# A hybrid decoder step: the side work beside the attention at other steps of the matrix engine's order, and two reciprocal roots on GpSimd

## The chip, the cores and the metric

The kernel runs on one core of a Trainium2 chip. The metric is the device time of one execution in microseconds (us). The kernel before took 2998.84 us (median of 3 runs, from 2991.91 to 3001.22 us). The engines are named as the profile names them: PE (TensorE's matmuls) with PEld (its weight loads), DVE (VectorE), ACT (ScalarE), POOL (GpSimd), and SP (SyncE), which here only issues DMAs, in the order of its program. Each engine works through its own list of instructions in order and waits at an instruction until what that one needs is there.

## The reference

One layer of a decoder for 2048 new prompt tokens and for a "sample" of 8 requests with 4 tokens each. Cut to what matters here:

```python
proj = rmsnorm(x, norm_attn_g) @ w_in               # 1024 -> 7 x 512
o_a  = HGRN2(qa, fa, ia)                            # gated recurrence, 4 heads of 128
o_a  = rmsnorm(o_a, hgrn_onorm_g) * silu(ga)        # needs 1/sqrt(mean(o_a^2) + EPS)
o_b  = dilated_attn(qb, kb, vb)                     # 8 heads of 64, windows (128,1), (512,4), (2048,16)
h    = x + concat(o_a, o_b) @ w_o
h    = h + ConvFFN(rmsnorm(h))                      # 1024 -> 2816 -> 1024
h    = h + sigmoid(rmsnorm(h) @ w_ple_gate) * (p @ w_ple_proj)
y    = rmsnorm(h)
```

The sample's tokens attend to a cached window of keys and values, and their recurrence starts from a stored state of 4 x 128 x 128 numbers for each request. Prompt and sample share the weights.

## The kernel before, in words

The program has three stages. First come the input projections for two blocks of tokens, with the prompt's recurrence (`hgrn_unit`, seven of its eight units) between them. Then comes the attention of the prompt, some 360 us, with the "side work" beside it. Last comes the trunk (output projection, channel mixer, embeddings), which takes the rest, about 1800 us.

The change touches the middle stage. The prompt's attention, `attn_phase`, is a generator that yields once per step. It goes through four pairs of heads (p = 0 to 3), and 160 units of 128 queries. Step x issues: the scores of unit x (lines 814 and 815: S from the query tile `qS` and the high and low part of the keys, `kH` and `kL`); on DVE the mask and the row's extreme (line 819), on ACT the exponential (line 820); at every second step, for the two units before, the transposes (line 827, `PT`), their copies on DVE or ACT (829) and the products with the values (839, `acc`). At planned steps it also issues the next pair's operands: `stage` (line 693, DMAs of a quarter of q and k), and and `stack`, which splits them: POOL rounds and subtracts (`qS` 152 and 704, `kL` 708), ACT casts (`kH` 707). `merge` (lines 745 to 778) reads row statistics back from memory, makes coefficients (DVE 753, 759; POOL 754 to 760; ACT 755, 765), writes and reads them back (`coef_d`, `cf`) and blends two results on POOL (775, 777).

The side work, `others()`, is a second generator with 92 steps: 31 of the recurrence's last unit (`hgrn_unit(..., apart=True)`), 44 of the sample's attention (`attn_sample`) and 17 of the sample's recurrence (`hgrn_sample`). `attn_sample` works on two groups of four requests. Each group streams 16 tiles (`skt`) from memory, through four buffers: eight of keys (line 944: four `kT_w`, four `kT_d`) and then eight of values (line 983: `v_w`, `v_d`), one tile per step, each with one product of PE (946, 986); between them stand a few steps of softmax and transposes without a tile. `hgrn_sample` loads one request's state per step (646), multiplies (659, 662), updates it on DVE (665) and writes it back (667).

A "turn" is one step of the attention, and after it, at some turns, one step of the side work. Within this loop PE's order is the order in which the code issues it (`manual_schedule` for PE). The other engines' order is made by a scheduler with a model of time; `first(side, 1)` issues the side's step with raised priority. Before the change the side stepped at every turn below 28 and then at every even turn, so its step n of 28 and more stood at turn 28 + 2 (n - 28): the sample's attention at turns 36 to 122, its recurrence at 124 to 156. The loop ends at turn 167.

The recurrence's unit ends with a norm: DVE makes the mean square `o_v` (line 573), `rsqrt_small` makes the reciprocal root of its 128 x 8 numbers by a bit trick and three rounds of Newton's method, eleven small DVE instructions (lines 104 to 109), DVE scales the two heads' output (579), PE transposes it (586). `hgrn_sample` does the same with one column of 128 (`hsv`, lines 671 to 677).

Of the kernel before, what the change touches and what calls it, by code (L numbers as in the profile page):

```python
# [11 lines left out]
F32 = mybir.dt.float32  # L12
# [4 lines left out]
ALU = mybir.AluOpType  # L17
# [31 lines left out]
def hymba_step_kernel(ctx: ExitStack, tc: tile.TileContext, I: dict, O: dict):  # L49
    nc = tc.nc  # L50
    V, A, G, PE, SP = nc.vector, nc.scalar, nc.gpsimd, nc.tensor, nc.sync

    const = ctx.enter_context(tc.tile_pool(name="const", bufs=1))
# [22 lines left out]
    ones = const.tile([128, 128], F32, name="ones")  # L76
    V.memset(ones, 1.0)

    mask = early.tile([128, 768], F32, name="mask")
    qT_s = early.tile([128, 4, NS], F32, name="qT_s")  # L80
    kT_s = early.tile([128, 4, NS], F32, name="kT_s")
# [14 lines left out]

    def f32(ap):
        return ap.bitcast(F32)

    def rsqrt_small(pool, v, shape):  # L100
        i = pool.tile(shape, I32, name="rs_i")
        y = pool.tile(shape, F32, name="rs_y")
        t = pool.tile(shape, F32, name="rs_t")
        V.tensor_scalar(i, v.bitcast(I32), 1, None, op0=ALU.logical_shift_right)
        V.tensor_scalar(y.bitcast(I32), i, -1.0, RSQRT_SEED, op0=ALU.mult, op1=ALU.add)
        for _ in range(3):
            V.tensor_mul(t, y, y)
            V.scalar_tensor_tensor(t, t, -0.5, v, op0=ALU.mult, op1=ALU.mult)
            V.scalar_tensor_tensor(y, t, 1.5, y, op0=ALU.add, op1=ALU.mult)
        return y  # L110
# [72 lines left out]
    def split_to(w, raw):  # L183
        A.copy(w[:, 0], raw)  # L184
        V.tensor_sub(w[:, 1], raw, f32(w[:, 0]))  # L185
        return w
# [3 lines left out]
    def down_weights(pool):  # L190

        tile_ = lambda: pool.tile([128, 512], F32, name="draw", bufs=8)
        for p in range(PAIRS):
            a = [tile_() for _ in range(4)]
            with tc.issue_after(recent[0].ins):
                for x, (i, j) in zip(a, itertools.product(range(2), repeat=2)):
                    SP.dma_start(x, I["w_down"][2 * p + j][:, 512 * i:512 * i + 512])
            for n, raw in factors(*a, tile_):
                w = split_to(pool.tile([128, 2, 512], F32R, name="dw", bufs=3), raw)
                SP.dma_start(f32(wd_d[p][n - 1]), f32(w))  # L200
                yield
# [22 lines left out]
    def in_phase(bi, tiles, shared, wp, ev, sm, pmm, pms, plv, po):  # L224
# [15 lines left out]
        def load_x(k, c0, cn):  # L240
            start = bi == 0 and c0 == 0
            cs = slice(c0, c0 + cn)
            g = gains[:, 0, k:k + 1]
            raw = ev.tile([128, 384], F32, name="xr", bufs=3)[:, :cn]
            SP.dma_start(raw, I["xT"][128 * k:128 * k + 128, t0 + c0:t0 + c0 + cn])
            A.activation(xh[k][:, cs], raw, AF.Copy, scale=g)  # L246
            V.scalar_tensor_tensor(xl[k][:, cs], raw, g, f32(xh[k][:, cs]), op0=ALU.mult, op1=ALU.subtract)  # L247
            if t0 + c0 + cn == NTOK:
                G.tensor_scalar(xs[:, k], raw[:, cn - NS:], g, 1.0, op0=ALU.mult, op1=ALU.mult)
            if k == 0:  # L250
                A.activation(ssq[:, cs], raw, AF.Square)
            else:
                sq = ev.tile([128, 512], F32, name="sg", bufs=2)[:, :cn]
                A.activation(sq, raw, AF.Square)
                (G if start else V).tensor_add(ssq[:, cs], ssq[:, cs], sq)
# [184 lines left out]
    def hgrn_unit(u, heads, S, ld, wk, sp, plv, po, pms, msk, diag, apart=False):  # L440
# [130 lines left out]
            yield  # L571
        v = sp.tile([128, 2, 4], F32, name="o_v")
        V.tensor_scalar(v, ssq, 1.0 / 128, EPS, op0=ALU.mult, op1=ALU.add)
        r = rsqrt_small(sp, v.rearrange("p h c -> p (h c)"), [128, 8])
        if apart:
            yield
        for i, h in enumerate(heads):
# [15 lines left out]
    def hgrn_sample(hp, pps):  # L593
# [76 lines left out]
        v = hp.tile([128, 1], F32, name="hsv")  # L670
        A.activation(o, ops, AF.Square, accum_out=v)
        V.tensor_scalar(v, v, 1.0 / 128, EPS, op0=ALU.mult, op1=ALU.add)
        r = rsqrt_small(hp, v, [128, 1])
        V.tensor_scalar(o, ops, r, None, op0=ALU.mult)
        yield
        pt = pps.tile([128, 4, 128], F32, name="s1")
# [897 lines left out]
    def pools(st, **kw):  # L1574
        def pool(name, bufs, **k):
            return st.enter_context(tc.tile_pool(name=name, bufs=bufs, reuse_waits="tile", **kw, **k))
        return pool

    in_st, hgrn_st, attn_st = [ExitStack() for _ in range(3)]
    pool = pools(in_st)  # L1580
# [11 lines left out]
    def hgrn(lo, hi, *psum, apart=False):  # L1592
        for i in range(lo, hi):
            heads = (0, 1) if i % 2 == 0 else (2, 3)
            yield from hgrn_unit(i // 2, heads, S, ld, wk, sp, *psum, msk, diag, apart)

    def first(gen, n):

        with tc.high_priority(AHEAD):
            return step(gen, n)  # L1600
# [17 lines left out]
    pool = pools(hgrn_st, side="right")  # L1618
    hc, ld, wk, sp = pool("h_c", 1), pool("h_l", 2), pool("h_w", 2), pool("h_s", 2)
# [19 lines left out]
    pool = pools(attn_st)  # L1639
# [5 lines left out]
    def others():  # L1645
        yield from hgrn(7, 8, from_pool(pps, "s1", "s2"), from_pool(pps, "s1"), from_pool(pps, "s2"), apart=True)
        for h in range(4):
            SP.dma_start(O["ps"][h], S[h])
        hgrn_st.close()
        with ExitStack() as st:  # L1650
            pool = pools(st)
            yield from attn_sample(pool("s_c", 1), pool("s_k", 4), pool("s_w", 1), pps)
        with ExitStack() as st:
            yield from hgrn_sample(pools(st)("hsp", 1), pps)

    side = others()
    with tc.manual_schedule(engines={mybir.EngineType.PE}):
        for turn in itertools.count(1):
            if next(main) == "last":
                break  # L1660
            if turn % 2 == 0 or turn < 28:
                first(side, 1)
        first(side, 1000)
    step(main, 1000)
# [4 lines left out]
    with ExitStack() as st:  # L1669
        pool = pools(st)  # L1670
# [9 lines left out]
        tr, tp, dw, ts, th, te, tw, hp = [pool(n, k) for n, k in (  # L1680
            ("tr", 7), ("tp", 6), ("dw", 6), ("ts", 1), ("th", 6), ("te", 2), ("tw", 44), ("thh", 8))]
# [143 lines left out]
```

## Time and profile before

| | before |
|---|---|
| time, median of 3 runs | 2998.84 us |
| the profiled execution's own time | 2996.88 us |
| its span, first to last instruction | 2995.1 us |
| PE busy | 2899.1 us (97 %) |
| DVE, ACT, POOL busy | 2163.4, 1318.4, 674.0 us |
| mean granted PE clock | 0.987 |

The profile is of one execution. Its page gives busy time by engine; the other views (windows, timeline, waits, groups by line, DMA) are answers of the same trace. In the timeline a row reads: start in us, duration in us, engine, line, operation, output<-input, tile sizes, how many instructions are merged; in brackets stands the idle time of the engine just before, and what ended it. In the windows view a row is a stretch of time with each engine's busy time (and its number of instructions), the granted PE clock as a share of full speed, the mean busy share of the 16 DMA engines and the GB/s that they moved. A DMA share at or above 1 means that packets queue up.

### The profile page before, as it was taken

Reading aid. Unit: us, or ns where it says so; the run is one execution under the profiler, and the core shown is the slowest. Engines: PE = TensorE matmul, PEld = TensorE weight load, DVE = VectorE, ACT = ScalarE, POOL = GpSimd, SP = SyncE. Lnnn points to the kernel's source line nnn. Section 1 sums busy time; section 2 is a strip of 40 time slices with the busy share of each in tenths; the row PEclk is TensorE's granted clock in tenths of the full one; section 3 lists DMA queues with packets and bytes.
Section 4 is the critical chain, followed back from the end, with each engine's and each line's share of the span. In section 5 each row is a group of like instructions: output and inputs, shape, how many; then the busy total and the mean of one; then the engine's idle time right before and its main releaser. Section 6 shows DMA issues by size and latency. Waiting matters only on the chain.

```text
span 2995.1 us, 52434 instructions
## 1 busy us (share of the span) xinstructions
PE 2899.1 (97%) x18895; PEld 2700.5 (90%) x18895; DVE 2163.4 (72%) x4717; ACT 1318.4 (44%) x2856; POOL 674.0 (23%) x792
## 2 busy tenths in 40 slices
PE   8999999999989898999999999999999999999998
PEld 8987789887777677999999999999999999999998
DVE  6656758657386467569987888766679777677777
ACT  5333423222276576335444444544444544444443
POOL 1443222212143563103443431000001000000000
PEclk9999999999999999999999999999999999999998
DMA  5898634324349996766766668777779777778773
GB/s 179 297 355 305 206 105 120 99 80 124 123 114 279 249 234 177 258 233 210 243 203 204 203 200 293 236 242 243 252 242 308 251 237 243 245 261 295 267 268 132
DMA packets 342036, 659.88 MB, mean 220 GB/s; under 512 B 62928, under 2 KB 134736, under 8 KB 339984
## 3 DMA queue, kind: packets, MB, share of 16 engines
q1 hardware_dynamic: 304928, 468.42, 49.0%
q0 software_dynamic: 33264, 121.13, 12.8%
q10 hardware_dynamic: 3584, 66.98, 6.2%
q8 instruction: 149, 2.44, 0.3%
q14 instruction: 111, 0.91, 0.1%
HBM read 509.46 MB, written 213.92 MB: 242 GB/s over the span
## 4 chain that ended last, share of the span: by engine, by line
PE 59%; issue 17%; DMA 10%; DVE 9%; POOL 2%; ACT 2%; SPq 1%; POOLq 0%; DVEq 0%; ACTq 0%
PE mm L146 13%; PE mm L148 13%; PE mm L147 13%; PE mm L348 2%; PE mm L349 2%; PE mm L350 2%; POOL w L1296 1%; DMA cf<-coef_d 1%; PE acc L839 1%; PE PT L827 1%; PE S L814 1%; DMA xr<-in_xT_dram 1%; PE lv L485 1%; DVE w L185 1%; DMA draw<-in_w_down_dram 1%
## 5 line engine op out<-in xcount | busy, mean ns | idle before, releaser
L147 PE MATMUL mm<-w 128*128 128x348 f32 (+3 forms) x3636 | 1166.1, 321 | 1.3 <-DVE w L1456 0.8
L146 PE MATMUL mm<-w 128*128 128x348 f32 (+3 forms) x3508 | 1108.7, 323 | 18.7 <-ACT s L1254 6.2
L148 PE MATMUL mm<-w 128*128 128x348 f32 (+3 forms) x3508 | 1117.3, 321 | 2.0 <-DVE w L185 2.0
L147 PEld LDWEIGHTS mm<-w 128*128 128x128 f32 x3636 | 684.1, 188 | 4.1 <-DVE w L1088 2.0
L146 PEld LDWEIGHTS mm<-w 128*128 128x128 f32 x3508 | 656.2, 188 | 26.6 <-ACT s L1254 8.7
L148 PEld LDWEIGHTS mm<-w 128*128 128x128 f32 x3508 | 659.0, 188 | 3.3 <-DVE w L185 2.6
L185 DVE TENSOR_TENSOR w<-raw,w 128x512 fp32r<-128x512 f32 x586 | 421.1, 723 | 176.2 <-ACT w L184 168.6
L184 ACT CAST w<-raw 128x512 fp32r<-128x512 f32 x586 | 360.9, 621 | 413.1 <-PE mm L148 288.8
L1296 POOL DMA_DIRECT2D w<-wd_d x231 | 124.3, 538 | 899.2 <-PE mm L148 793.4
L1312 DVE TENSOR_TENSOR h<-h,mm 128x348 f32<-128x348 f32 (+1 forms) x504 | 247.7, 507 | 44.8 <-PE mm L148 43.5
L820 ACT ACTIVATE P<-P,st 128x256 f32<-128x256 f32 (+3 forms) x256 | 134.0, 526 | 60.0 <-DVE st L819 56.4
L1254 ACT COPY s<-mm 128x348 f32<-128x348 f32 (+1 forms) x198 | 88.0, 445 | 152.2 <-PE mm L148 151.9
L819 DVE CUSTOM_DVE_ANT_0 P<-S,mask 128x256 f32<-128x256 f32 (+3 forms) x256 | 104.4, 448 | 62.0 <-PE S L815 40.2
L348 PE MATMUL mm<-wh,xh 128*128 128x512 f32 x352 | 140.8, 403 | 0.1
L349 PE MATMUL mm<-wl,xh 128*128 128x512 f32 x352 | 140.7, 401 | 0.2 <-DVE wl L271 0.2
L350 PE MATMUL mm<-wh,xl 128*128 128x512 f32 x352 | 140.3, 399 | 0.0
L146 PE MATMUL mm<-xh,wh 128*128 128x384 f32 (+2 forms) x384 | 124.6, 329 | 8.0 <-ACT xh L246 5.2
L148 PE MATMUL mm<-xh,wl 128*128 128x384 f32 (+2 forms) x384 | 124.4, 328 | 4.2 <-DVE wl L271 4.2
L147 PE MATMUL mm<-xl,wh 128*128 128x384 f32 (+2 forms) x384 | 125.0, 328 | 1.2 <-DVE xl L247 1.2
L185 DVE TENSOR_TENSOR dw<-draw,dw 128x512 fp32r<-128x512 f32 x77 | 75.3, 981 | 54.0 <-ACT dw L184 53.6
L152 POOL TENSOR_SCALAR wh<-wraw 128x512 fp32r<-128x512 f32 x96 | 75.3, 798 | 133.3 <-PE mm L147 41.6
L814 PE MATMUL S<-kH,qS 128*128 128x256 f32 (+3 forms) x256 | 98.6, 400 | 6.7 <-DVE st L819 4.2
(346 smaller groups left out, 5053.2 us busy)
## 6 DMA issues: line engine op xcount, KB each, us to landing
w<-wd_d POOLq DMA_DIRECT2D x231, 512.0 KB, 5.5
wd_d<-dw SPq DMA_DIRECT2D x77, 512.0 KB
out_sk_dram<-in_cache_k_dram ACTq DMA_DIRECT2D x56, 584.0 KB
out_sv_dram<-in_cache_v_dram ACTq DMA_DIRECT2D x56, 584.0 KB
raw<-in_w_gate_dram SPq DMA_DIRECT2D x110, 256.0 KB
raw<-in_w_up_dram SPq DMA_DIRECT2D x110, 256.0 KB
wraw<-in_w_in_dram SPq DMA_DIRECT2D x104, 256.0 KB
raw<-w_gate_d SPq DMA_DIRECT2D x88, 256.0 KB
```

The source lines that it names most:

```text
L146: PE.matmul(ps, lhsT=wh, rhs=xh, start=first, stop=False, skip_group_check=read)
L147: PE.matmul(ps, lhsT=wh, rhs=xl, start=False, stop=False, skip_group_check=read)
L148: PE.matmul(ps, lhsT=wl, rhs=xh, start=False, stop=last, skip_group_check=read)
L184: A.copy(w[:, 0], raw)
L185: V.tensor_sub(w[:, 1], raw, f32(w[:, 0]))
L348: PE.matmul(ps, lhsT=xh[k][:, js], rhs=wh, start=k == 0, stop=False)
L349: PE.matmul(ps, lhsT=xh[k][:, js], rhs=wl, start=False, stop=False)
L350: PE.matmul(ps, lhsT=xl[k][:, js], rhs=wh, start=False, stop=k == NK - 1)
L814: PE.matmul(s[:, w * i:w * i + w], lhsT=bl.q(hh), rhs=bl.k(kH, hh), start=True, stop=False)
L820: A.activation(pe, pe, AF.Exp, bias=mn, scale=-1.0, accum_out=st[:, bl.r, hh, 0:1])
L1296: G.dma_start(t, wd_d[p][n - 1])
L1312: V.tensor_add(o, o, acc[m][:, :H])
```

## The change

Three edits. `rsqrt_pow` makes the reciprocal root with one POOL instruction, a power with exponent -0.5 from a constant tile `root`; it is used in `hgrn_sample` and in the recurrence's unit that runs beside the attention (`apart`), while the first seven units keep `rsqrt_small`. And the side work steps, from turn 28 on, at three of seven turns instead of one of two, and above turn 136 at five of seven.

```diff
+    root = const.tile([128, 1], F32, name="root")
+    G.memset(root, -0.5)
...
+    def rsqrt_pow(pool, v, shape):
+        y = pool.tile(shape, F32, name="rs_y")
+        G.tensor_tensor(y, v, root.to_broadcast(shape), op=ALU.pow)
+        return y
...
-        r = rsqrt_small(sp, v.rearrange("p h c -> p (h c)"), [128, 8])
+        r = (rsqrt_pow if apart else rsqrt_small)(sp, v.rearrange("p h c -> p (h c)"), [128, 8])
...
-        r = rsqrt_small(hp, v, [128, 1])
+        r = rsqrt_pow(hp, v, [128, 1])
...
-            if turn % 2 == 0 or turn < 28:
+            if turn < 28 or turn % 7 in (0, 2, 4) or (turn > 136 and turn % 7 in (1, 5)):
                 first(side, 1)
```

By this rule the sample's attention stands at turns 37 to 137 (before 36 to 122) and its recurrence at 138 to 161 (before 124 to 156). The steps of the recurrence's last unit that hold the root stand where they stood. The same PE instructions are issued in another order, and before and behind the attention stage no engine's order changes. From `rsqrt_small` on, the changed kernel's lines are counted higher by 7: the old line 819 is now 826.

The first place is DVE's list at the norm of the recurrence's last unit. Before, the last twelve rows up to the scaling of the two heads (`at`):

```order
L105 TENSOR_SCALAR rs_y<-rs_i 128x8
L829 COPY pt<-PT 128x512
L107 TENSOR_TENSOR rs_t<-rs_y 128x8
L108 SCALAR_TENSOR_TENSOR rs_t<-rs_t,o_v 128x8
L109 SCALAR_TENSOR_TENSOR rs_y<-rs_t,rs_y 128x8
L107 TENSOR_TENSOR rs_t<-rs_y 128x8
L108 SCALAR_TENSOR_TENSOR rs_t<-rs_t,o_v 128x8
L109 SCALAR_TENSOR_TENSOR rs_y<-rs_t,rs_y 128x8
L107 TENSOR_TENSOR rs_t<-rs_y 128x8
L108 SCALAR_TENSOR_TENSOR rs_t<-rs_t,o_v 128x8
L109 SCALAR_TENSOR_TENSOR rs_y<-rs_t,rs_y 128x8
L579 TENSOR_TENSOR at<-at,rs_y 128x512 x2
```

The same place of the change, from the mean square `o_v` on (the ISA rows are the masks and extremes of the attention's scores):

```order
L580 TENSOR_SCALAR o_v<-o_ssq 128x8
L826 ISA P,st<-S,mask 128x256
L826 ISA st 128x1
L826 ISA P,st<-S,mask 128x256
L826 ISA st 128x1
L826 ISA P,st<-S,mask 128x256
L826 ISA st 128x1
L826 ISA P,st<-S,mask 128x256
L826 ISA st 128x1
L836 COPY pt<-PT 128x512
L586 TENSOR_TENSOR at<-at,rs_y 128x512 x2
L594 TENSOR_TENSOR hg<-s_9590,hg 128x512
```

The eleven small instructions are gone, and the scaling stands behind the attention's own rows alone. On POOL one row is new there:

```order
L711 TENSOR_TENSOR qS<-stage,qS 64x512 x2
L761 TENSOR_TENSOR w<-mn,st 128x16
L104 TENSOR_TENSOR rs_y<-o_v,root 128x8
L715 TENSOR_TENSOR kL<-stage,kH 128x4x128 x2
L764 TENSOR_TENSOR wl<-w,st 128x16
```

It stands ahead of the two key differences `kL` of the next pair.

The second place is SP's list where the last two quarters of the fourth pair's operands (`stage`) are fetched. Before:

```order
L983 DMA skt<-in_v_d_dram 96x4x512
L745 DMA st<-stat_d 128x4x4
L693 DMA stage<-qT_d 64x2x512 x2
L737 DMA v<-v_d 32x4x128 x8
L693 DMA stage<-kT_d 64x2x512 x2
L734 DMA v<-v_d 128x4x128
L737 DMA v<-v_d 32x4x128 x2
L693 DMA stage<-qT_d 64x2x512 x2
L737 DMA v<-v_d 32x4x128 x2
L745 DMA st<-stat_d 128x4x4
L693 DMA stage<-kT_d 64x2x512 x2
```

And of the change:

```order
L990 DMA skt<-in_v_w_dram 128x4x512
L752 DMA st<-stat_d 128x4x4
L700 DMA stage<-qT_d 64x2x512 x2
L744 DMA v<-v_d 32x4x128 x8
L700 DMA stage<-kT_d 64x2x512 x2
L741 DMA v<-v_d 128x4x128
L744 DMA v<-v_d 32x4x128
L700 DMA stage<-qT_d 64x2x512 x2
L744 DMA v<-v_d 32x4x128
L990 DMA skt<-in_v_d_dram 96x4x512
L744 DMA v<-v_d 32x4x128 x2
L700 DMA stage<-kT_d 64x2x512 x2
```

Before, the sample's last tile (`v_d`) is issued ahead of these quarters; now four of its tiles are still to come there, the first of them between the last quarter's queries and keys.

## The prediction

> **What bounds the kernel now.** I began with the page: which engine is full, and what the chain that ended last consists of.
>
> ```profile
> PE 2899.1 (97%) x18895; PEld 2700.5 (90%) x18895; DVE 2163.4 (72%) x4717; ACT 1318.4 (44%) x2856; POOL 674.0 (23%) x792
> PE 59%; issue 17%; DMA 10%; DVE 9%; POOL 2%; ACT 2%; SPq 1%; POOLq 0%; DVEq 0%; ACTq 0%
> ```
>
> PE bounds the whole, but DMA has a tenth of the chain. Since the change moves nothing outside the attention, I cut that stage into windows by turns. (Turns are counted by their first scores, L814, in the timeline; the windows are turns 33 to 60, 61 to 84, 85 to 104, 105 to 124, 125 to 156.)
>
> ```profile
> core 0: us, PE busy (x) PEld busy (x) DVE busy (x) ACT busy (x) POOL busy (x), PEclk, DMA share, GB/s
> 905.11:960.60 55.49, 53.97 (x501) 41.49 (x499) 35.49 (x133) 40.11 (x117) 19.66 (x27) 1.00 1.04 292
> 960.60:1024.30 63.70, 55.41 (x464) 37.26 (x460) 30.28 (x119) 36.20 (x109) 37.31 (x44) 0.92 1.03 250
> 1024.30:1065.50 41.20, 38.38 (x349) 28.75 (x345) 25.92 (x76) 26.45 (x68) 8.78 (x9) 1.00 1.03 276
> 1065.50:1111.50 46.00, 43.59 (x379) 32.16 (x375) 26.61 (x107) 32.97 (x102) 38.13 (x47) 0.90 0.88 216
> 1111.50:1178.60 67.10, 63.53 (x603) 53.39 (x601) 49.42 (x195) 38.61 (x122) 25.86 (x35) 0.99 0.64 171
> ```
>
> The DMA share is full as long as the sample's attention streams (to about 1091 us), and has room behind it. What would PE alone need? Two undisturbed pairs of turns, with one tile of the sample and with none:
>
> ```profile
> 1086.93 0.39 PE L814 MATMUL S<-kH,qS 128*128 128x256 f32 x1
> 1090.97 0.39 PE L814 MATMUL S<-kH,qS 128*128 128x256 f32 x1
> ...
> 1178.57 0.37 PE L814 MATMUL S<-kH,qS 128*128 128x256 f32 x1
> 1181.60 0.39 PE L814 MATMUL S<-kH,qS 128*128 128x256 f32 x1
> ```
>
> A bare pair of turns takes 3.03 us, a tile 1.01 us more. So turns 61 to 84 (12 pairs, 12 side steps) need 48.5 us and took 63.7: 15.2 lost. Turns 105 to 124 (10 pairs, 9 side steps) need 39.4 and took 46.0: 6.6 lost. Turns 33 to 60 (14 pairs, 12 tiles: 54.5) and 85 to 104 (10 and 10: 40.4) lose 1.0 and 0.8 only.
>
> How it is lost, the timelines of ACT and PE show:
>
> ```profile
> 1010.71 2.12 ACT L707 CAST kH<-stage 128x512 fp32r<-128x512 f32 x2 [5.89 <-DMA stage<-kT_d]
> 1099.40 2.14 ACT L707 CAST kH<-stage 128x512 fp32r<-128x512 f32 x2 [2.67 <-DMA stage<-kT_d]
> ...
> 1013.38 1.17 PE L827 MATMUL PT<-c_ident,P 128*128 128x128 f32 x4 [4.04 <-ACT P L820]
> 1102.10 1.18 PE L827 MATMUL PT<-c_ident,P 128*128 128x128 f32 x4 [1.00 <-ACT P L820]
> ```
>
> ACT stands at the cast of the next pair's keys, whose transfer is late in a full queue; the exponentials are queued behind the cast, and PE's transposes wait for them. Of 5.89 us at ACT, 4.04 reach PE, so about 1.85 are hidden. Then the clock goes, too:
>
> ```profile
> 899.19:904.20 5.01, 5.01 (x26) 4.68 (x28) 4.25 (x14) 2.08 (x8) 2.66 (x5) 0.50 0.66 207
> 1013.40:1020.20 6.80, 6.38 (x34) 3.46 (x34) 0.69 (x1) 4.24 (x18) 2.56 (x3) 0.50 1.11 197
> 1101.10:1102.20 1.10, 0.10 (x1) 0.10 (x2) 0.51 (x4) 1.10 (x4) 1.03 (x1) 0.98 0.98 292
> 1102.20:1112.40 10.20, 9.77 (x56) 7.82 (x57) 2.50 (x12) 5.87 (x26) 7.87 (x12) 0.50 0.64 168
> ```
>
> Half clock costs about half of such a stretch: 2.5, 3.4 and 5.1 us.
>
> **Part A, the root of the recurrence's last unit.** The timelines of DVE, PE and POOL, in this order:
>
> ```profile
> 891.74 0.39 DVE L573 TENSOR_SCALAR o_v<-o_ssq 128x8 f32<-128x8 f32 x1
> 892.05 0.42 DVE L819 CUSTOM_DVE_ANT_0 P<-S,mask 128x256 f32<-128x256 f32 x1
> 892.40 0.98 DVE L104 TENSOR_SCALAR rs_i<-o_v 128x8 int32<-128x8 int32 x1
> ...
> 895.21 0.68 DVE L829 COPY pt<-PT 128x512 f32<-128x512 f32 x1
> 898.44 1.29 DVE L579 TENSOR_TENSOR at<-at,rs_y 128x512 f32<-128x512 f32 x2
> ...
> 899.19 1.11 PE L586 MATMUL s<-c_ident,at 128*128 128x128 f32 x4 [4.80 <-DVE at L579]
> ...
> 893.43 0.23 POOL L754 TENSOR_TENSOR w<-mn,st 128x16 f32<-128x16 f32 x1
> 893.73 3.01 POOL L708 TENSOR_TENSOR kL<-stage,kH 128x512 fp32r<-128x512 f32 x2
> 897.18 0.20 POOL L758 TENSOR_TENSOR mn<-wl 128x8 f32<-128x8 f32 x1
> ```
>
> PE waits 4.80 us for the scaling. Without the eleven instructions DVE has four score rows of 0.35 us (892.05 to 892.40, start to start) from 892.05 on, to 893.44, then the copy, 0.68: it is at the scaling at 894.12, if the root is there. The root starts on POOL behind L754, at 893.73. No power is in the trace. Its nearest row is the 128x8 instruction at 0.20 us, the lower end; for the upper end I take one of the two key differences, 1.5 us (3.01 for two), the costliest POOL work of this place. I take 0.5, near the small row: 894.23, with the semaphore 894.3. The scaling released PE 0.75 us after its start (898.44 to 899.19), so PE goes on at 895.05: 4.1 us saved (4.3 and 3.1 at the ends). The half clock that followed, 2.5 us, goes too if the 0.7 us that is left of the wait does not bring it. Sum **-6.5**, from -7 to -3. The key differences behind the power move by its 0.5 us. They are operands of the second pair, whose scores begin at turn 41, some ten us later, and that time hides them; without it PE would wait those 0.5 us. That DVE has eleven instructions less I cost at nothing: PE, not DVE, is the fuller engine in every window above.
>
> [...]
>
> **Part B, the sample's attention at three of seven turns.** What a tile costs the DMA engines comes from the DMA view of 905.1 to 1186.6 us (packets, MB and share of the 16 engines of the queue; then issues of one kind and KB each):
>
> ```profile
> q1 hardware_dynamic: 60837, 65.40, 89.0%
> skt<-in_v_w_dram SPq DMA_DIRECT2D x8, 1024.0 KB
> skt<-in_v_d_dram SPq DMA_DIRECT2D x8, 768.0 KB
> ```
>
> 89.0% of 281.5 us for 65.40 MB is 3.83 us per MB; a mean tile (0.92 MB, keys are of the same two sizes) is 3.5 us. Turns 61 to 84 hold 12 side steps now and 10.3 then: 1.7 tiles or 6.0 us less. Where DMA is the bound (share 1.03), the stretch gets shorter by that; the 1.7 products of PE come later, at 1.01 us each, where PE sets the pace: **-4.3**. In turns 105 to 124 it is the other way. There the last tile is issued at turn 108 now; tiles run four ahead of their use, so then four tiles of 0.79 MB are fetched at turns 114 to 121, and some two or three more fall into this stretch: 6 to 9 us of DMA on top of 0.88 x 46.0 = 40.5. That is 46.5 to 49.5 for 46.0 us: it becomes full. I take **+1.5**. The keys' casts of the last pair (the ones at 1099) are the ones that wait for it; queued behind them are the exponentials, and for these PE waits. Bounds of B: -17, if all that turns 33 to 104 lose (1.0 + 15.2 + 0.8) went, and +9, if one more cast of the last pair is hit as the one at 1010 (4.04 + 3.4, and the 1.5).
>
> **Part C, the end.** The sample's last transpose waits for its root, and the trunk's first weights wait behind its state:
>
> ```profile
> 1178.48 0.33 PE L677 MATMUL s<-c_ident,hso 128*128 128x128 f32 x1 [1.41 <-DVE hso L674]
> 1180.25 4.07 SPq L1011 DMA_DIRECT2D raw<-in_w_o_dram  x3
> 1192.80 0.59 PE L146 MATMUL mm<-w 128*128 128x348 f32 x2 [3.44 <-ACT w L1087]
> ```
>
> The first wait goes but for one power: -1. The weights are issued at 1180.25, at turn 158; now the last state is written at turn 159 and they come behind it. PE has 3.44 us of wait there, on ACT, which casts weights first: +1 (0 to +2). The recurrence at five of seven turns puts the same work closer; PE had no wait on its states, and DMA has room (0.64): 0, at most +2.
>
> **The sum**: -6.5 - 4.3 + 1.5 - 1 + 1 = -9.3 against the profiled execution's 2996.88 us: 2987.6. The median stands 2 us above that execution; against it 2989.5. I say **2989**.
>
> **Rivals.** (1) *DMA stops being the bound.* For: 15.2 us of loss hang on a share of 1.03, and one tile in seven less may be enough to let every cast find its keys. Against: each quarter of a pair still stands behind tiles in SP's list. Then all 15.2 + 1.8 us go, less 1.7: -6.5 - 15.3 = -22, 2977. (2) *The stall only moves.* The last pair pays what the third stops paying and 2 us more: -6.5 + 2 = -4.5, 2994. SP's list speaks for it, with a tile between the last queries and keys; against it, only two or three tiles more are fetched there. (3) *Slower: the last pair's casts.* If three of its casts wait over 1.85 us more than now for their keys, each costs 4.04 + 3.4 us as at 1010, less the 6.1 paid there already: +16.1 - 6.5 = +9.6, 3008. It decides at a landing later than that; against it, DMA begins the stretch with 12% free. [...]
>
> **How the numbers follow.** Chances: the forecast 0.50, for its two larger terms each rest on a row; (1) 0.16, (2) 0.17, (3) 0.11, (4) 0.06. The forecast's own range is 2981 to 2998 (A from -7 to -3, B from -10 to +2, C from -1 to 0). 0.3% is 9 us, about what a measurement of this kernel can tell from none: 2989.8 is the bound below, and the forecast lies on it: faster are half of the forecast, 0.26, and (1), 0.42 together; slower (3) and a little of (4), 0.12; the same 0.46. The range takes in (1) and (4) but not (3): 2976 to 3004.
>
> **What would show it.** A: the wait before the transposes of `at` under 1 us and clock 1.00 behind it; the power's row near 0.5 us. B: turns 61 to 84 at 58 us or so, DMA share at 1.0 on to turn 124; the casts of the fourth pair's keys waiting longer than 2.67 us. C: the wait before the trunk's first product near 4 us. A power of several us, or a wait of 4 us or more on the exponentials behind turn 105, would make it wrong.

## The result, and the profile after

The changed kernel takes 3010.98 us (median of seven runs, 3003.63 to 3017.18) against 2998.84 us: a ratio of 1.0045, 95% interval 1.0033 to 1.0058. It is some 12 us slower, where 10 us less were forecast, and 7 us above the range. The profiled execution took 3017.18 us, 6 above its median; that of before stands 2 below its own. So single profiles are compared here with care, and a reading counts where several profiles agree on it.

The chain that ended last, of the page of the changed kernel, by engine:

```profile
PE 76%; DMA 9%; DVE 8%; ACT 2%; issue 2%; POOL 1%; SPq 1%; DVEq 0%; POOLq 0%; ACTq 0%
```

DMA and DVE have nearly as much of it as before (10 and 9%), and PE and "issue" together 78% for 76%, so the change is not seen there. The windows by turns tell more. These are turns 29 to 36, 37 to 60, 61 to 84, 85 to 104, 105 to 124 and 125 to 159 (up to the first scores of turn 159) of the changed kernel, and behind them the last stretch of the kernel before:

```profile
core 0: us, PE busy (x) PEld busy (x) DVE busy (x) ACT busy (x) POOL busy (x), PEclk, DMA share, GB/s
894.80:917.80 23.00, 17.50 (x135) 15.34 (x133) 20.86 (x56) 16.49 (x50) 17.16 (x22) 0.78 0.72 229
917.80:969.20 51.40, 49.15 (x427) 37.42 (x425) 27.99 (x105) 32.62 (x94) 17.51 (x21) 0.97 1.08 230
969.20:1036.20 67.00, 53.57 (x438) 39.13 (x436) 29.61 (x116) 38.46 (x115) 38.23 (x45) 0.87 1.01 236
1036.20:1078.20 42.00, 39.07 (x316) 28.78 (x312) 23.11 (x69) 20.34 (x57) 10.27 (x9) 1.00 0.97 270
1078.20:1120.40 42.20, 40.03 (x401) 30.52 (x401) 26.39 (x115) 36.49 (x110) 30.04 (x39) 1.00 0.98 222
1120.40:1201.50 81.10, 74.30 (x674) 59.23 (x672) 51.10 (x190) 41.68 (x131) 27.25 (x38) 0.96 0.59 163
...
1111.50:1181.60 70.10, 66.53 (x634) 56.05 (x632) 51.78 (x205) 40.36 (x129) 25.86 (x35) 0.99 0.62 166
```

Turns 105 to 124 are shorter than before (42.2 for 46.0 us); turns 61 to 84, where 58 were expected, took 67.0; and the last stretch took 81.1 against 70.1 us before, which is half of the 20 us between the two profiles. Part A is in the first window. The timelines of POOL, DVE and PE there:

```profile
896.97 0.22 POOL L761 TENSOR_TENSOR w<-mn,st 128x16 f32<-128x16 f32 x1
897.15 1.68 POOL L104 TENSOR_TENSOR rs_y<-o_v,root 128x8 f32<-128x8 f32 x1
898.82 3.45 POOL L715 TENSOR_TENSOR kL<-stage,kH 128x512 fp32r<-128x512 f32 x2
...
898.87 3.95 DVE L586 TENSOR_TENSOR at<-at,rs_y 128x512 f32<-128x512 f32 x2 [1.18 <-POOL rs_y L104]
...
900.93 1.11 PE L593 MATMUL s<-c_ident,at 128*128 128x128 f32 x4 [2.98 <-DVE at L586]
912.95 0.39 PE L821 MATMUL S<-kH,qS 128*128 128x256 f32 x1 [2.53 <-DVE st L826]
```

The power took 1.68 us where 0.5 was assumed. The scaling behind it, 0.65 us apiece before, took 1.97 apiece, for it now runs at the same time as POOL's key differences. So PE still waited 2.98 us, and some 12 us later it waited another 2.53 us, for DVE's masks. Behind turn 128 there is a chain that the prediction did not have:

```profile
1127.03 2.48 POOL L782 TENSOR_TENSOR o<-o,cf 128x512 f32<-128x512 f32 x2 [8.09 <-DMA cf<-coef_d]
1129.55 0.69 DVE L784 TENSOR_TENSOR o<-o,o 128x512 f32<-128x512 f32 x1 [6.65 <-POOL o L782]
1130.98 0.51 PE L821 MATMUL S<-kH,qS 128*128 128x256 f32 x1 [3.50 <-DVE st L826]
```

`merge` reads its coefficients back from memory; POOL waits for them, DVE's addition waits for POOL, the masks are queued behind that addition, and PE waits for the masks. There are two more of PE's waits in the last stretch, the first of the same kind, the second at the first product of the sample's recurrence. The last two rows are the closing products of the sample's attention, which came in turns 105 to 124 before:

```profile
1153.10 0.57 PE L821 MATMUL S<-kH,qS 128*128 128x384 f32 x1 [0.97 <-DVE st L826]
1158.54 0.44 PE L622 MATMUL s<-hsq,hsF 128*32 128x32 f32 x8 [2.04 <-POOL hsF L613]
...
1141.46 1.06 PE L998 MATMUL s<-v_s,sPTn 32*32 32x512 f32 x8
1145.61 0.96 PE L1004 MATMUL s<-ssel,som 128*128 128x16 f32 x8
```

### The profile page after: what moved, and what is told of

Its sections match the earlier page's. It is cut to its first block, busy times and chain, and to the rows that moved or that the text cites. A ratio compares the mean times of both kernels' runs of the same rounds, so it can differ in the third digit from the quotient of the medians.

```text
span 3015.4 us, 52417 instructions
## 1 busy us (share of the span) xinstructions
PE 2909.6 (96%) x18895; PEld 2710.3 (90%) x18895; DVE 2154.9 (71%) x4695; ACT 1318.9 (44%) x2856; POOL 676.8 (22%) x795
## 4 chain that ended last, share of the span: by engine, by line
PE 76%; DMA 9%; DVE 8%; ACT 2%; issue 2%; POOL 1%; SPq 1%; DVEq 0%; POOLq 0%; ACTq 0%
PE mm L153 19%; PE mm L155 19%; PE mm L154 19%; PE mm L356 2%; PE mm L355 2%; PE mm L357 2%; DMA cf<-coef_d 2%; PE acc L846 1%; PE PT L834 1%; PE S L821 1%; DVE h L1319 1%; DMA draw<-in_w_down_dram 1%; DMA stage<-kT_d 1%; DMA xr<-in_xT_dram 1%; PE lv L492 1%
## 5 line engine op out<-in xcount | busy, mean ns | idle before, releaser
L821 PEld LDWEIGHTS S<-kH,qS 128*128 128x128 f32 x256 | 65.7, 257 | 61.2 <-DVE st L826 30.7
```

The source lines that it names most:

```text
L821: PE.matmul(s[:, w * i:w * i + w], lhsT=bl.q(hh), rhs=bl.k(kH, hh), start=True, stop=False)
```

## The experiments

The kernels e1 to e18 were timed in five rounds beside runs of the kernel before on the same chip; the ratios are against those. The columns of turns are lengths in us in each run's one profile, between first scores (125-159 ends at the first scores of turn 159); "end" is from there to the trunk's first product; "512 B" is the mean time in ns of the 512-byte packets between 826 and 1190 us, from the trace's packet records (the attention of the changed kernel runs on behind 1190, so its 38 is not quite comparable).

```
run                        ratio (95% interval)     29-36  37-124 125-159  end   512 B
before                     1                        21.6   198.6   70.1   11.2   33
the change                 1.0045 (1.0033-1.0058)   23.0   202.6   81.1   13.5   38
e1_pow_only                1.0036 (1.0020-1.0053)   22.6   210.8   69.6   11.3   36
e2_turns_only              1.0044 (1.0032-1.0056)   21.6   194.8   82.3   17.5   33
e3_adds_on_pool            1.0066 (1.0050-1.0083)   22.5   191.7   79.1   12.3   37
e4_before_adds_on_pool     1.0008 (0.9994-1.0023)   21.6   196.4   72.7   11.3   32
e5_power_unit_only         1.0059 (1.0036-1.0082)   22.8   210.8   70.6   11.7   36
e6_power_sample_only       1.0018 (1.0004-1.0032)   21.6   201.2   66.6   10.4   36
e7_power_qb_on_act         1.0037 (1.0025-1.0049)   18.9   211.2   68.5   11.5   36
e8_five_of_seven_only      1.0071 (1.0053-1.0089)   21.2   203.3   77.1   12.5   36
e9_constant_only           1.0048 (1.0032-1.0065)   21.6   207.4   69.2   11.1   36
e10_dead_power             1.0045 (1.0029-1.0060)   24.7   200.8   69.1   11.9   36
e11_heads_swapped          1.0009 (0.9997-1.0021)   22.4   197.9   69.2   12.5   33
e12_three_then_four        1.0048 (1.0034-1.0063)   21.2   197.4   73.0   16.2   37
e13_constant_64            1.0011 (0.9999-1.0024)   21.6   202.2   68.0   11.7   35
e14_power_64               1.0030 (1.0017-1.0043)   22.9   200.9   69.5   11.8   35
e15_change_64              1.0042 (1.0027-1.0058)   22.6   189.4   80.4   12.2   35
e16_before_tiles_64        1.0003 (0.9992-1.0015)   21.6   198.7   70.8   11.5   33
e17_constant_again         1.0032 (1.0020-1.0044)   21.6   201.7   69.8   11.0   36
e18_values_moved           1.0015 (1.0003-1.0027)   21.6   202.9   69.6   10.5   36
```

### The two parts alone

The changed kernel with the old turns (e1, shown), and the kernel before with the new turns (e2, the reverse edit):

```diff
-            if turn < 28 or turn % 7 in (0, 2, 4) or (turn > 136 and turn % 7 in (1, 5)):
+            if turn % 2 == 0 or turn < 28:
```

> The change without its new turns: both roots by the power, the side steps on even turns as before. Theory M (the loss comes from the new turns alone, through the merge's adds on VectorE, which wait for coefficients that land late): this is no slower than before, 2992 to 2999 us, the wait ahead of the transposes of at shorter than 4.80 us, VectorE's wait at the merge's adds near the 20.7 us of before. Theory P (the power costs: its first row is 1.68 us, and the scaling behind it took 1.97 us a piece instead of 0.65): 3002 to 3008 us, half or more of the 12 us lost.

> The change without the power: both roots by VectorE's eleven instructions, the side steps on the new turns. Theory M: the whole loss and a little more, 3011 to 3017 us, VectorE's wait at the merge's adds near 40 us. Theory P: 3003 to 3008 us. Theory K (the keys' casts alone pay, the third rival of the prediction): also 3011 or more, but the loss stands at the waits for the exponentials, not at the waits for the scores' statistics.

Each part alone loses nearly what the whole loses, 0.36% and 0.44%; theory M, which gave all of it to the turns, falls, and the parts do not add. In the run with the powers alone, PE waits 2.98 us at the transposes instead of 4.80, and then 4.55 us at the scores of turn 35, where it did not wait before:

```profile
899.09 3.95 DVE L586 TENSOR_TENSOR at<-at,rs_y 128x512 f32<-128x512 f32 x2 [1.19 <-POOL rs_y L104]
901.15 0.66 PE L593 MATMUL s<-c_ident,at 128*128 128x128 f32 x4 [2.98 <-DVE at L586]
906.22 3.82 DVE L940 COPY qb<-qT_s 64x32 f32<-64x32 f32 x6
912.56 0.58 PE L821 MATMUL S<-kH,qS 128*128 128x256 f32 x1 [4.55 <-DVE st L826]
```

In the run with the turns alone the sample's last transposes wait for VectorE's root, which the denser steps have brought closer to them (1.41 us before):

```profile
1202.58 0.48 PE L677 MATMUL s<-c_ident,hso 128*128 128x128 f32 x1 [6.58 <-DVE hso L674]
```

### The merge's additions on GpSimd

In the changed kernel (e3) and in the kernel before (e4):

```diff
-            (G if p == 3 else V).tensor_add(parts[1], parts[1], parts[0])
+            G.tensor_add(parts[1], parts[1], parts[0])
```

> The changed kernel, but the merge's add of the first three pairs is issued on GpSimd, behind its multiplications, as that of the fourth pair already is; VectorE then waits for no coefficient. Theory M: the waits of 2.19, 4.69, 1.70, 1.46 and 3.50 us at the scores go, with the half clock behind them: 2997 to 3003 us. If the o buffers that ScalarE copies into come free too late, a part of it comes back as a wait on ScalarE: 3003 to 3008 us. Theories K and P: 3009 to 3013 us, no change against the changed kernel.

> The kernel before with the same add on GpSimd, as the control. Theory M: VectorE's 20.7 us of waits were hidden to less than 2 us there, so 2995 to 3000 us, within 0.15% of before. If the add's engine were worth something by itself (theory K or P with another cause of the gain), it would gain here as much as in the changed kernel, 5 us or more.

VectorE's waits for coefficients went, as meant, and so did the five waits at the scores that hung on them; yet the kernel got no faster than the changed one (1.0066). Its profile is of its fastest execution (3002.58 us, 10 below its median) and still shows the wait for the fourth pair's first keys, 6.63 us against 5.54 in the changed kernel:

```profile
998.63 2.10 ACT L714 CAST kH<-stage 128x512 fp32r<-128x512 f32 x2 [9.53 <-DMA stage<-kT_d]
1001.28 0.96 PE L834 MATMUL PT<-c_ident,P 128*128 128x128 f32 x3 [6.63 <-ACT P L827]
```

The coefficients are not the only ones that come late; ScalarE's cast waits 9.53 us for keys. And ahead of the transposes of turn 122 PE waits 4.42 us, where it waited 1.04 in the changed kernel. To take these additions off VectorE did not make the kernel faster, and in the kernel before it changed nothing (1.0008): theory M's remedy falls, and that the late coefficients cause the loss is not shown.

### The power, place by place

Power in the unit alone (e5), in the sample's recurrence alone (e6), and both with the copies into `qb` on ScalarE (e7); all with even turns:

```diff
# e5
-        r = rsqrt_pow(hp, v, [128, 1])
+        r = rsqrt_small(hp, v, [128, 1])
# e6
-        r = (rsqrt_pow if apart else rsqrt_small)(sp, v.rearrange("p h c -> p (h c)"), [128, 8])
+        r = rsqrt_small(sp, v.rearrange("p h c -> p (h c)"), [128, 8])
# e7
-                V.tensor_copy(qb[rows, :, p, c:c + 4], qT_s[rows, p].rearrange("p (b t) -> p b t", t=4))
+                A.copy(qb[rows, :, p, c:c + 4], qT_s[rows, p].rearrange("p (b t) -> p b t", t=4))
```

> The power in the recurrence's last unit alone, the sample's root by VectorE, side steps on even turns. Theory V (VectorE becomes the bound behind the root: its scaling takes 1.97 us a piece beside GpSimd's key differences, so what PE gains in turns 29 to 32 it pays in turns 33 to 36, and all later staging stands differently): turns 29 to 36 take 22.4 to 23.0 us against 21.6 of before, and the kernel takes as long as with both powers, +6 to +12 us against before. Theory S (the loss of the run with both powers comes from the sample's root at the end): -4 to 0 us against before.

> The power in the sample's recurrence alone. Theory V: -2 to 0 us against before (the wait of 1.41 us ahead of the sample's last transposes goes), turns 29 to 36 unchanged at 21.6. Theory S: +6 us or more.

> Both powers, side steps on even turns, and the eight copies into qb (3.5 to 4.8 us of VectorE just behind the scaling) on ScalarE. Theory V: the wait of 4.55 us at the scores of turn 33 to 36 shrinks to under 1.5, these eight turns take 18.5 to 20.5 us, and against the run with both powers the kernel gains 2 to 4 us if only these eight turns count, 8 or more if the later loss hangs on them. If ScalarE or GpSimd hold PE there instead: no change against the run with both powers.

Turns 29 to 36 answer to theory V in every profile: 22.5 to 23.0 us in the six with the power in the unit (e7 aside), 21.2 to 21.6 in the eleven that leave this place as it was, and 18.9 with the copies taken off VectorE. So VectorE is the bound there, and the power makes these turns some 1 us longer. But 1 us is not 11 or 18 (the losses of e1 and e5), and the 2.7 us that e7 gained there against before did not arrive at the end (1.0037). The sample's root did what was forecast (the wait of 1.41 us is gone from e6's profile), and yet e6 is slower. Something that all these kernels share was missing from both theories.

### The density of the side steps

> The sample's power, the attention on even turns as before, and from turn 123 on five of seven turns for its recurrence. Theory D (density: a step's transfers and its GpSimd work no longer fit between it and the next, so PE waits at the steps): +3 to +8 us against before, with a wait of some 2 us at the first level's product and PE waits at later steps, turns 125 to 159 over 73 us against 70.7. Theory T (the tail: the new turns lose because three of seven pushes six tiles of the attention out of a stretch that DMA bounds into one that PE bounds): -2 to +2 us, turns 125 to 159 within 2 us of 70.7.

> The sample's power, three of seven turns as in the change, but from turn 137 on four of seven (to turn 167, the loop's last) in place of five. Theory D (density of the recurrence's steps costs): turns 125 to 159 at 72 to 76 us against 80 to 83 with five of seven, and the kernel 3 to 8 us faster than the changed kernel, +4 to +9 against before. Theory T (the tail of the attention's tiles in turns 125 to 137 costs): turns 125 to 140 still at 36.5 to 38.5 us against 33.1 of before, and the kernel as slow as the changed one, +10 to +14.

```diff
# e8 (with the sample's power)
+            if turn < 28 or (turn % 2 == 0 if turn < 123 else turn % 7 in (0, 1, 2, 4, 5)):
# e12 (with the sample's power)
+            if turn < 28 or turn % 7 in (0, 2, 4) or (turn > 136 and turn % 7 == 6):
```

Five of seven alone made turns 125 to 159 longer, 77.1 us against 66.6 in e6, which was timed on the same chip, and 1.0071 against 1.0018: theory D. PE waits there for what a closer step finds unfinished, 6.1 us in all, the longest for VectorE's update of a state; the clock was 0.92, against 0.99 and no wait over 0.4 us in e6:

```profile
1124.00 0.44 PE L622 MATMUL s<-hsE,hsF 128*32 128x32 f32 x8 [1.42 <-DVE hsF L434]
1154.21 2.04 PE L669 MATMUL s<-hsvm,hskt 32*128 32x128 f32 x8 [3.42 <-DVE hsn L672]
1172.68 0.33 PE L684 MATMUL s<-c_ident,hso 128*128 128x128 f32 x1 [1.26 <-DVE hso L681]
```

Four of seven shortened the last stretch to 73.0 as D expected, but the steps that no longer fit came behind it: 16.2 us to the trunk instead of some 12, and the whole no faster (1.0048), as T expected. Neither theory has it alone. Steps put closer cost; steps put later cost too.

### The constant's place

The kernel before with nothing of the change but the tile `root` and its memset (e9), and the same with 64 bytes a partition (e13). A tile takes its bytes in each of 128 partitions, and in the built program the tiles lie one behind the other:

```diff
+    root = const.tile([128, 1], F32, name="root")
+    G.memset(root, -0.5)
# e13
+    root = const.tile([128, 16], F32, name="root")[:, :1]
```

> The kernel before with the constant tile of the change and its memset, and no power: every engine's list but that of GpSimd, which has one memset more at the start, is the list of before. Control for where the tiles lie in memory and for the measurement. All theories: 0, within 0.15% of before; if it is slower by 0.2% or more, the tiles' places cost, and that much of the power's loss is theirs.

> The constant tile alone again, but 64 bytes a partition instead of 4 (which take 32): all later tiles move by 64 bytes, so that those of the attention start at multiples of 64 bytes as before. Theory L (places: a start at 32 bytes beyond a multiple of 64 makes the transfers of 512 bytes slower): 0, within 0.15% of before, with 512-byte packets at 33 ns and some 3.86 us of the queue's time per MB in the attention. Theory G (the memset or the tile itself): +0.3 to +0.6% as with 4 bytes.

A tile that nothing uses costs 0.48%. The lists of all engines are those of before but for one memset at the start. What differs is where the tiles lie: the four bytes take 32, and in the built program's addresses the attention's values `v`, which started at multiples of 256 bytes, now start 32 beyond one, with `stage`, `cf` and `o`; the sample's `skt`, 32 beyond such a multiple before, starts 64 beyond one. At 64 bytes the loss is gone to within the measurement (0.11%, -0.01 to 0.24%), so neither the memset nor the tile itself carries it. The runs e1, e3, e5 to e8, e10 and e12 all have the tile of four bytes, so a part of what they lose can be its own. The queue's row of the DMA view, 905 to 1180 us (packets, MB, share of 16 engines), in the order before, e9, e13 and e18 below:

```profile
q1 hardware_dynamic: 59330, 64.55, 89.9%
```
```profile
q1 hardware_dynamic: 58312, 63.81, 91.7%
```
```profile
q1 hardware_dynamic: 59363, 64.62, 90.8%
```
```profile
q1 hardware_dynamic: 59401, 62.96, 89.9%
```

Share times 275 us by MB: 3.83, 3.95, 3.86 and 3.93 us per MB. With the tile at 32 bytes the queue needs 3% more time for the same bytes, in a stage that it fills to nine tenths, and 1% more with 64. But the 512-byte packets, which e13 was expected to bring back to 33 ns, took 35.3 there, against 35.5 in e17 (the tile of four bytes once more, below) and 35.9 in e9: their time does not tell the slow kernels from the fast one. Which tiles it is, and whether it comes again on another chip:

> The kernel before with 32 bytes more in one tile of the sample's attention, so that its tiles skt, whose rows are 1.5 and 2 KB, start at multiples of 64 bytes too; all lists are those of before. Theory L by the packets (those of 1.5 KB took 89 to 91 ns at both places): 0, within 0.15%. If the places of these tiles cost as those of the attention do: 0.1 to 0.4% faster than before.

> The constant tile of 4 bytes alone once more, beside the next run on one chip. Theory L (places): +0.3 to +0.5% again, 512-byte packets in the attention at 36 ns. If the first run of it was an outlier: under +0.2%.

> The kernel before with 32 bytes ahead of the six buffers of the values (v, loaded in rows of 512 bytes) and 32 behind them: these alone start at 32 bytes beyond a multiple of 64, all else moves by 64 bytes or not at all; every list is that of before but for two memsets on GpSimd. Theory L by the 512-byte packets: +0.3 to +0.5%, as much as the constant tile in the same call, packets at 36 ns. If other tiles are meant (stage, cf, o): 0 to +0.15%, packets at 33 to 34 ns.

```diff
# e18, in the kernel before
         vals = {}
+        pad = wk.tile([128, 8], F32, name="pad1", bufs=1)
+        G.memset(pad, 0.0)
...
         for f in todo.pop(-1):
             f()
+        pad = wk.tile([128, 8], F32, name="pad2", bufs=1)
+        G.memset(pad, 0.0)
# e16
-        neg = cp.tile([128, new], F32, name="sneg")
+        neg = cp.tile([128, new + 8], F32, name="sneg")[:, :new]
```

It came again, with 0.32% (0.20 to 0.44%). The place of the sample's tiles does not matter alone (e16). The values alone, loaded in rows of 512 bytes, bring the packets to 36 ns and 0.15% of loss (0.03 to 0.27%), which is no more than the measurement can tell from e13's 0.11%, in which `cf` and `o` moved by the same 64 bytes. So the place of the tiles is the cause of the constant's loss, but which tiles, and by which step of a transfer, stays open; `stage`, `cf` and `o` were not moved by 32 alone. The mean time of a 512-byte packet was 33 ns with the values at a multiple of 256 bytes (before), 36 at 32 beyond it (e9, e17, e18) and 35 at 64 beyond it (e13); why, no run shows.

### Is it the scheduler's new order?

A power whose result nobody reads (e10), and the scaling of the two heads issued the other way round (e11); each makes the scheduler place dozens of DMAs anew:

```diff
# e10
         r = rsqrt_small(sp, v.rearrange("p h c -> p (h c)"), [128, 8])
+        if apart:
+            rsqrt_pow(sp, v.rearrange("p h c -> p (h c)"), [128, 8])
# e11
-        for i, h in enumerate(heads):
+        for i, h in (list(enumerate(heads))[::-1] if apart else enumerate(heads)):
```

> The kernel before, and beside VectorE's root, which is still the one used, one power on GpSimd in the recurrence's last unit, whose result nobody reads. PE's list is that of before; 36 rows of SyncE's list and 13 of VectorE's stand elsewhere, for the scheduler, which has a model of time, places them anew. Theory V (VectorE behind the root): turns 29 to 36 stay at 21.6 us, and the kernel within 0.15% of before, for the scaling does not move. Theory R (the edits lose because the scheduler's new list for SyncE serves the transfers worse, whatever the edit's own time): +3 to +12 us, with turns 65 to 68 near 14 us as in the runs with the power in the unit.

> The kernel before with the scaling of the two heads issued in the other order: no work is added or taken, but the scheduler gives SyncE 66 rows, GpSimd 46 and VectorE 76 at other places. Theory R: off the time of before by 3 to 12 us, slower likelier than faster, with the difference in turns 61 to 124 at the loads of tiles, coefficients or keys. Theory V: within 0.15% of before.

The kernel with 66 of SyncE's rows elsewhere and no other work is within 0.21% of before, so this new order, at least, does not carry a loss of 0.4%. e10 is as slow as e9, whose tile it has: the dead power adds nothing that can be measured at the end, though turns 29 to 36 take 24.7 us where theory V expected 21.6. It shows the price of neighbours plainly. Lines of VectorE's root (114 and 116 here), beside POOL's key differences and behind them:

```profile
894.53 2.98 POOL L717 TENSOR_TENSOR kL<-stage,kH 128x512 fp32r<-128x512 f32 x2
894.64 1.42 DVE L116 SCALAR_TENSOR_TENSOR rs_y<-rs_t,rs_y 128x8 f32<-128x8 f32 x1
896.10 1.44 DVE L114 TENSOR_TENSOR rs_t<-rs_y 128x8 f32<-128x8 f32 x1
...
897.57 0.17 DVE L115 SCALAR_TENSOR_TENSOR rs_t<-rs_t,o_v 128x8 f32<-128x8 f32 x1
897.77 0.17 DVE L116 SCALAR_TENSOR_TENSOR rs_y<-rs_t,rs_y 128x8 f32<-128x8 f32 x1
897.97 0.17 DVE L114 TENSOR_TENSOR rs_t<-rs_y 128x8 f32<-128x8 f32 x1
```

One instruction takes 0.17 us behind POOL's key differences and 1.42 beside them, about the length of one of POOL's two (2.98 us together). The scaling's 1.97 us apiece beside them in the changed kernel, for 0.65 behind them in the kernel before, are of the same kind.

### The parts with the places of before

Both powers (e14) and the whole change (e15), with the constant at 64 bytes:

> Both powers, side steps on even turns, with the constant at 64 bytes. Theory L: 0.3 to 0.5% faster than the run with both powers, that is -0.15 to +0.1% of before: the power's own effect is the +1 us of turns 29 to 36 less the 1.4 us at the sample's root. Theory R (the scheduler's list, 103 rows of SyncE elsewhere): +0.2 to +0.5%, and turns 65 to 68 again near 14 us.

> The whole change with the constant at 64 bytes. Theory L and a loss of the turns by themselves: faster than the changed kernel, but slower than before by 0.15 to 0.35% (the run with the new turns alone lost 0.44%, of which some 5 us were the wait of 6.58 us for the sample's root, which the power shortens). If the turns cost nothing beside the places: -0.1 to +0.1%. If the places cost nothing here: +0.45% as the changed kernel.

e14 stands 0.19% above e13, the same tile without the powers: some 6 us, of which turns 29 to 36 show 1.3. Its 1.0030 is above what theory L allowed and within what theory R did (the scheduler's order; its sign, turns 65 to 68, took 11.6 us, for 8.7 before and 15.0 in e1), so R is not ruled out for these 6 us. e15 stands at 1.0042, practically the changed kernel: its stretch of turns 37 to 124 is the shortest of all (189.4 us, in a profile 4 us below the run's median), and its last one is 80.4. So with the new turns the constant's place does not show in the time any more; the turns' loss stands by itself, and the three causes do not add.

No run was faster than the kernel before.

## Why the prediction was wrong

**Part A was -6.5 us and measured +0.8 to +1.3** (turns 29 to 36, the six profiles with the power there). Its first half was right: the eleven instructions went, the scaling came earlier, and PE's wait fell from 4.80 to 2.98 us. Three terms were mis-sized or missing. The power took 1.68 us for 0.5, beyond the upper end of 1.5. The scaling's price, 0.75 us to PE's start, was taken from a place where POOL was idle and used at a place where POOL was not; the row that would have told it was in the trace of before, where line 107 of the root took 0.95 us beside POOL (at 895.81) and 0.20 behind it (at 897.20). And "PE, not DVE, is the fuller engine in every window" was the wrong test for these twelve us, in which VectorE was the bound: PE got ahead and waited for the masks. The sum also takes it that the 0.7 us left of the wait bring no half clock, which is 2.5 of its 6.5 us. That was an assumption, and the trace of before does not settle it: the clock was 1.00 behind PE's waits of 0.86 and 1.41 us (from 1135.25 and 1178.48 on) and 0.50 behind one of 1.00 us (from 1102.20 on). In the changed kernel it was 0.50 behind the wait of 2.98 us (900.90 to 907.00).

**Part B's own stretch was about right, and its sum was not.** Turns 61 to 84 were forecast at 58 us: 59.2, 57.9 and 58.0 in e2, e3 and e12, though 62.0 in e15 and 67.0 in the changed kernel's profile. The step that failed is "the 1.7 products of PE come later, at 1.01 us each". It counted only what these 24 turns give up. Over all turns from 37 on, six steps of the sample's attention (turns 126, 128, 130, 133, 135 and 137) come to stand behind turn 124, where DMA has room (share 0.59) and PE sets the pace: three tiles at 1.01 us, the closing products with 0.99 and 0.81, and a last step without a product, 4.8 us. (The prediction's 39.4 us for turns 105 to 124 counts the same closing steps as tiles.) The second failing step is the 0 to +2 us for five of seven. Turns 125 to 159 took 79.1 to 82.3 us in the four profiles with both, against 70.1. In the changed kernel 3.50, 0.97 and 2.04 us are waits of PE there (the merge's coefficients twice, then the recurrence's first product, whose operands a denser step reaches too early), against 0.55, 0.42, 0.86 and 1.41 before: 3.3 us more. And the clock was 0.96 for 0.99 (0.78 in the 7.9 us behind the wait of 3.50 us), which by estimate is some 2.5 us of the 81.1. These three make 10.6 of the 11.0 us. The waits of the third rival, the last pair's casts, were not what decided: turns 105 to 124, where +1.5 was forecast, were 3.8 us shorter in the changed kernel, and between 5.0 shorter and 1.3 longer in e2, e3, e12 and e15.

**Part C.** The sample's root did go (0.58 us for 1.41). The trunk's first product waited 5.11 us for 3.44, within the term's 0 to +2. In the forecast's own range C goes from -1 to 0, which is narrower than its terms; they allow up to +3.

**A term that was missing** is the constant's. `root` was described ahead of the prediction, and the sum has no term for it. In the kernel before it costs 0.32 to 0.48%, 10 to 14 us, more than any term of the sum. But it is not what made the forecast miss: without its shift by 32 bytes the whole change still loses 0.42% (e15), and the turns without the tile lose 0.44% (e2).

**Rivals.** That the stall only moves was thought of the last pair's transfers, where it did not happen; in form it is what happened at part A (the gain is paid back some 12 us later) and in e3. The third rival had nearly the size (3008) but not the place. The fourth, that the power is slow, was ruled out: the power's two rows took 1.68 and 0.57 us in the changed kernel, and no row read in another run (e1, e6, e10, e14) took longer.

What stays open: why three causes of 0.2 to 0.5% each make 0.45% together, and some 4 us of the powers' 0.19%, which no window of the profiles holds and which the scheduler's order may carry. That the constant shows with the old turns and not with the new ones was measured once (e15 against the changed kernel), and its reason was not looked for further.

## What to carry to other kernels

When an edit adds a tile, however small, compare the addresses of the tiles behind it before and after; a pad of 64 bytes told this apart from the edit itself (here 0.48% of loss with the tile of 4 bytes, 0.11% with 64). When work moves from VectorE to GpSimd, price both engines' neighbours at the new place, from rows in which the two ran side by side (here 1.42 us beside POOL's key differences for an instruction that took 0.17 behind them). And when work is thinned out in a stretch that DMA bounds, follow each displaced step of the whole stretch to where it is done, and charge it there at that place's price.

## What the runs showed of the hardware that was not expected

The power took 1.67 to 1.68 us for 128x8 (the changed kernel, e1, e10, e14) and 0.57 to 0.58 for 128x1 (the changed kernel, e1, e6, e14); by an estimate from these two sizes, (1.68 - 0.57) / 7, that is some 0.16 us a column. Packets of 1.5 KB, which only the sample's tiles have, did not get dearer or cheaper with the place of their tile in a way that the runs tell apart (89 and 92 ns in before and e13 at 32 bytes beyond a multiple of 64, 85, 91 and 93 in e16, e9 and e17 at one); those of 512 bytes did, 32 to 33 ns with the values at a multiple of 256 bytes (before, e2, e4, e11, e16) and 35 to 37 (38 in the changed kernel) with them 32 or 64 beyond one; yet 64 beyond cost the kernel nothing that could be measured (e13). And half clock followed a wait of 2.98 us (0.50 behind it) but not one of 1.04 us (1.00 behind it) at nearly the place (turn 122) where before it had followed one of 1.00 us (0.50 behind it). These are windows of the changed kernel, ahead of and behind each:

```profile
897.90:900.90 3.00, 0.05 (x2) 0.00 (x0) 2.03 (x2) 3.00 (x12) 3.00 (x3) 0.88 0.73 179
900.90:907.00 6.10, 6.07 (x33) 5.41 (x34) 5.96 (x17) 2.96 (x9) 5.86 (x9) 0.50 0.68 199
1112.60:1113.70 1.10, 0.08 (x1) 0.01 (x1) 0.90 (x4) 1.10 (x5) 1.02 (x2) 1.00 1.02 218
1113.70:1118.00 4.30, 4.28 (x37) 3.05 (x37) 1.89 (x13) 3.41 (x16) 3.02 (x4) 1.00 1.11 214
```
